# One encoder step on one core: row factors, the squares' output, the band norm's loads and block 2's operand splits are moved

## The chip, the cores and the metric

The kernel runs on one core of one Trainium2 chip. The time is device microseconds (us) of one execution of the whole program; beside it one execution was taken with the hardware profiler. TensorE (PE in the profile) does the matrix products, ScalarE (ACT), VectorE (DVE) and GpSimd (POOL) do elementwise work, and SyncE (SP) issues the DMA transfers. Each engine executes its own instructions in a fixed order and waits on semaphores for the others.

## The reference

A one-layer encoder step over 2048 prompt rows and 32 sample rows of width 1024:

```python
a = rmsnorm(x, g_attn)
qa, ka, va, qb, kb, vb = split(a @ w_in)           # two groups of heads, 512 columns each
oa = diff_attention(qa, ka, va)                    # group A: 4 heads, two maps each, chunk-causal
ob = band_attention(qb, kb, vb)                    # group B: 8 heads, band of 9 chunks of 64 rows
h = x + concat(rmsnorm(oa, subln_g) * 0.2, rmsnorm(ob, out_norm_b)) @ w_out
h = h + square(relu(rmsnorm(h, g_mlp) @ w_up)) @ w_down
h = h + sigmoid(h @ w_ple_gate) * (p @ w_ple_proj)
y = rmsnorm(h, g_final)
```

All values are float32; keys and values are outputs too.

## The kernel before

**Tiling.** The rows are cut into four blocks of 512 (block 3 has 544, the 32 sample rows being its tail). Activations lie transposed: 128 features on the partitions, rows along the free dimension. Every operand of a product is kept as two parts, a first part (rounded by ScalarE, `hi`) and a second part (the remainder, `lo`, by GpSimd or VectorE); `split` at line 178 makes the two, and `mm3` at line 210 does three matmuls per product (lines 216 to 218). In the profile a weight's first part is `wh` or `piece`, its second part `wl` or `piece`, and the raw weight from memory `wr`.

**Order.** The Python program traces instructions one after the other. A planner then fixes each engine's order: it runs a simulated clock and gives each engine the ready instruction that was traced earliest (a block under `high_priority` counts as traced earlier). So a matmul of a later stage fills a gap of an earlier one, and the attention of one block has the projection of another beside it. What the planner takes for ready is simulated; on the chip an engine that reaches an instruction too early waits there, with everything behind it. `tc.issue_after(ins)` puts the instructions that its block traces on the engine of `ins` behind `ins`. `weave` (line 100) and `weave2` (line 89) trace one generator and let another do a step after each of its steps. Tiles with one `tag` share a ring of `bufs` buffers.

**Preparation (`prep`, line 359).** For each tile of 128 rows (a "turn"): load `x`; square it with a sum over the row (line 371, which writes its unused squares into `xt`); transpose the eight 128x128 squares of `x` through PSUM tiles `xp` (line 378); write the two parts `aH` and `aL` (lines 383 and 384); copy the transposes to `xt` (line 387), which goes to memory as `xT`; from the row sums make the factor `rcol` (`rsqrt`, lines 223 to 231), transpose it by TensorE (line 392, `rp`) and copy it to `rbt` (line 393), by which queries and keys are scaled later. Blocks 0 and 1 are prepared at the start, beside group A's value tiles (`vtile`, `vps`); blocks 2 and 3 later, under raised priority, beside group B's projection and attention. There `x`, `xt` and `st` have one buffer each, and the PSUM tiles `xp`, `rp`, `vps` and `qps` share a ring of two banks.

**Band norm (`onorm`, line 927).** The factor of the norm of `ob`: load the four 128-row pieces `oraw` of the block from memory (`raw_o`, a ring of three buffers), square them on ScalarE (lines 934 and 936), add on GpSimd; split the sum (`sh`, `sl`), sum over partitions with TensorE (`css`, line 1100), take the inverse root, store it as `rB`. For blocks 0 and 1 it is woven into `proj_a` (37 steps, counted from 0) at the steps that `ONP` gives: block 0 at steps 28 and 34, block 1 at 29 and 35. The later use is in `oload` (line 940), which loads `rB` for the pieces 4 to 7 of the out-projection's operand `oact`. For blocks 2 and 3 `ONQ` gives the steps.

**Operands of block 2 (`cparts`, line 1008).** The MLP of blocks 2 and 3 uses seven combinations of the quarters of the normed activation (`b11`, `b21`, `b22`, `t1` to `t4`). For each of four `k`: two loads `tmp`, two scalings (line 1021), three splits, four additions on VectorE (lines 1033 to 1036), four splits of the sums; all of that in one step of the generator. Two steps are woven into `outproj(3)`, two into `gate(0)` (whose products are `gps` and `pps`), followed there by the first step of `mlp7(2)`, which makes its first weight combinations (`lead`). The same code for block 3, `cstage`, already does the last four splits of `k` after the loads of `k + 1`.

Of the kernel before, what the change touches and what calls it, by code (L numbers as in the profile page):

```python
# [20 lines left out]
P = 128  # L21
# [54 lines left out]
JA0 = [(0, 1), (2, 3)]  # L76
JA1 = [(4, 5), (6, 7, 8)]
JB = [(0, 1), (2, 3), (4, 5), (6, 7, 8)]
ONP = (28, 1, 6)
ONQ = (8, 1, 1)  # L80
PW = 272


# [5 lines left out]
def weave2(main, sides, at):  # L89
    n = 0  # L90
    for _ in main:
        for i, side in enumerate(sides):
            if n in (at[0] + i * at[1], at[0] + i * at[1] + at[2]):
                next(side, None)
        n += 1
    for side in sides:
        drain(side)


def weave(main, side, step, i=0, n=1):  # L100
# [43 lines left out]
class Kern:  # L144
# [33 lines left out]
    def split(self, hi, lo, raw, hi_eng="act", lo_eng="pool"):  # L178
        nc = self.nc
        if hi_eng == "act":  # L180
            nc.scalar.activation(hi, raw, AF.Copy)  # L181
        else:
            nc.vector.tensor_copy(hi, raw)
        if lo_eng == "pool":
            self.pool_tt(lo, raw, hi.bitcast(F32), ALU.subtract)
        else:
            nc.vector.tensor_tensor(lo, raw, hi.bitcast(F32), op=ALU.subtract)
# [171 lines left out]
    def prep(self, b, acts, pp, mm, tag, first=None):  # L359
        nc = self.nc  # L360
        aH, aL = acts[b]
        for i, (c0, n) in enumerate(toks(b)):
            t0 = 512 * b + c0
            x = pp.tile([P, D], F32, tag="x", name="x")
            self.dma(x[:n], self.xsrc(t0, n))
            if first is not None:
                first()
                first = None
            xt = pp.tile([P, 8, P], F32, tag="xt", name="xt")
            st = pp.tile([P, 1], F32, tag="st", name="st")  # L370
            nc.scalar.activation(
                xt[:n].rearrange("p a b -> p (a b)"), x[:n], AF.Square, accum_out=st[:n]
            )
            for h in range(2):
                xp = mm.tile([P, 4, P], F32, tag=tag, name="xp")
                for k in range(4):
                    kk = 4 * h + k
                    nc.tensor.transpose(xp[:, k, :n], x[:n, kk * P : kk * P + P], self.ident[:n, :n])
                for k in range(4):
                    kk = 4 * h + k  # L380
                    g = self.g_attn[:, kk : kk + 1]
                    hi, lo = aH[:, kk, c0 : c0 + n], aL[:, kk, c0 : c0 + n]
                    nc.scalar.activation(hi, xp[:, k, :n], AF.Copy, scale=g)
                    nc.vector.scalar_tensor_tensor(
                        lo, xp[:, k, :n], g, hi.bitcast(F32), op0=ALU.mult, op1=ALU.subtract
                    )
                nc.vector.tensor_copy(xt[:, 4 * h : 4 * h + 4, :n], xp[:, :, :n])
            self.dma(self.xT[:, :, t0 : t0 + n], xt[:, :, :n])
            r = self.rcol[:n, 4 * b + i : 4 * b + i + 1]
            self.rsqrt(pp, st[:n], 1, 1.0 / D, EPS, nc.vector, "r1", n, out=r)  # L390
            rp = mm.tile([P, 512], F32, tag=tag, name="rp")
            nc.tensor.transpose(rp[:, :n], r.broadcast_to([n, P]), self.ident[:n, :n])
            nc.scalar.activation(self.rb[b][:, c0 : c0 + n], rp[:, :n], AF.Copy)
            yield

    def ktok(self, b):
        if b < 3:
# [526 lines left out]
        self.dma(t, self.oT[:, k, t0 : t0 + n])  # L924
        return t

    def onorm(self, b, wk, ps, tag, dst):
        nc = self.nc
        n, t0 = BN[b], 512 * b
        sq = wk.tile([P, BLK], F32, tag="acc", bufs=2, name="sqacc")[:, :n]  # L930
        for k in range(4, 8):
            raw = self.raw_o(wk, k, t0, n)
            if k == 4:
                nc.scalar.activation(sq, raw, AF.Square)
            else:
                nc.scalar.activation(raw, raw, AF.Square)
                self.pool_tt(sq, sq, raw, ALU.add)
        yield from self.colnorm2(sq, b, 1.0 / 512, wk, ps, tag, dst, [])

    def oload(self, b, wk, up, out):  # L940
# [67 lines left out]
    def cparts(self, b, wk, cs, out, r):  # L1008
        nc = self.nc
        n, t0 = BN[b], 512 * b  # L1010
        m = n // 2
        names = ("b11", "b21", "t2", "t1", "t3", "b22", "t4")
        ops = {x: [cs.tile([P, 4, 272], F32R, tag="cs", name="cs")[:, :, :m] for _ in range(2)] for x in names}
        out[b] = ops
        for k in range(4):
            c = []
            for i in range(2):
                tmp = wk.tile([P, BLK], F32, tag="tmp", bufs=self.nt, name="tmp")[:, :n]
                kk = k + 4 * i
                self.dma(tmp, self.hS[:, kk, t0 : t0 + n])  # L1020
                nc.vector.scalar_tensor_tensor(
                    tmp, tmp, self.g_mlp[:, kk : kk + 1], r, op0=ALU.mult, op1=ALU.mult
                )
                c.append((tmp[:, :m], tmp[:, m:]))
            (b11, b12), (b21, b22) = c
            raw = {"b11": b11, "b21": b21, "b22": b22, "t3": b22, "t1": b12, "t2": b11, "t4": b21}

            def parts(*which):
                for x, e in which:
                    self.split(ops[x][0][:, k], ops[x][1][:, k], raw[x], "act", e)  # L1030

            parts(("b11", "pool"), ("b21", "dve"), ("b22", "dve"))
            nc.vector.tensor_tensor(b22, b22, b12, op=ALU.subtract)
            nc.vector.tensor_tensor(b12, b12, b11, op=ALU.subtract)
            nc.vector.tensor_tensor(b11, b22, b11, op=ALU.add)
            nc.vector.tensor_tensor(b21, b21, b11, op=ALU.subtract)
            parts(("t2", "dve"), ("t1", "dve"), ("t3", "dve"), ("t4", "pool"))
            yield

    def cstage(self, b, up, out, r):  # L1040
        nc = self.nc
# [414 lines left out]
    def run(self):  # L1456
        tc, nc, a = self.tc, self.nc, self.a
        with ExitStack() as top:
# [24 lines left out]
            with ExitStack() as x:  # L1483
                pp = opened(x, "pp0", 3, side="right")
                wv = opened(x, "wv0", 1, side="right")
                acts = {b: self.actpair() for b in HALVES[0]}
                for b in HALVES[0]:
                    self.rows(b, sg)
                units = []

                def first():
                    self.consts(cp)

                ring = Rings((ps_s, "s"), (ps_t, "tp"))
                todo = [(b, i) for b in HALVES[0] for i in range(4)]
                gen = (y for b in HALVES[0] for y in self.prep(b, acts, pp, ring, "s", first if b == 0 else None))
                next(gen)
                units.append(self.vunits(0, 0, pool=wv))
                next(gen)
                units.append(self.vunits(0, 1, pool=wv))  # L1500
                self.gains(cp)
                for b, i in todo:
                    for c in range(2):
                        self.vtile(b, i, 0, c, units[c], acts, sg, mm)
                    next(gen, None)
            ppx = ExitStack()
            pp = opened(ppx, "pp", 1)
            self.rawp = Rings((self.wp, "wr"), (opened(ppx, "wr3", 1), "wr"))
# [43 lines left out]
                for b in HALVES[1]:  # L1552
                    yield from self.proj((b,), 0, acts, sg, mm, tp, vs=(), gs=range(GS, 4))

            weave2(proj_a(), [self.onorm(b, wq, mm, "mm", self.rB) for b in HALVES[0]], ONP)
            s12.close()
            self.small = False
            sq_ = ExitStack()
# [65 lines left out]
            with ExitStack() as x:  # L1624
                act = Sized(opened(x, "acth", 2), BLK, True)
                weave(self.outproj(2, wk, oa[2], md, acc[2]), self.oload(3, wk, act, oa), 1, 0, 2)
                g = self.outproj(3, wk, oa[3], md, acc[3])
                made = []
                hp = self.hparts(0, wk, up, made)
                for _ in range(3):  # L1630
                    next(g)
                    next(hp, None)
                r2 = self.colnorm(acc[2][0], 2, 1.0 / D, wk, mm, "mm", None)
                c = self.cparts(2, wk, cs, ops, r2)
                weave(g, islice(c, 2), 1)
            hh = [opened(top, f"hh{i}", 1) for i in range(2)]
            h = hload(hh[0], BLK, 0)
            g = self.gate(0, h, up, None, md, wk, made[0])
            next(g)
            box = []  # L1640
            m = self.mlp7(2, hh[1], box, ops[2], wk, up, mm, md)
            weave(g, self.along(c, m), 1)
            f = self.final(0, h, up, fk, mm)
            for _ in range(2):
                next(m)
# [66 lines left out]
```

## Time and profile before

| | |
|---|---|
| median of 3 runs | 3151.15 us (3149.49 to 3156.91) |
| the profiled execution: its time, its span | 3146.42 us, 3144.6 us |
| mean granted TensorE clock | 0.985 |
| busy: VectorE, ScalarE, GpSimd | 1897.6, 1878.1, 1847.6 us (60%, 60%, 59%) |
| memory traffic | 539.27 MB, 172 GB/s over the span |

A row of the waits reads "engine, tile and line, what released it: total us, times, longest us". A row of the timeline reads "start, length, engine, line, operation, output and inputs, count, and in brackets the idle time before it with its releaser". A row of the windows gives, for a stretch, its length, then busy time and number of instructions of PE, PEld, DVE, ACT and POOL, the granted TensorE clock, the DMA share and GB/s. A row of a tile's or line's instructions gives the least, median and greatest length in ns.

### The profile page before, as it was taken

The page shows a single profiled execution, that of the slowest core. Times are in us where ns is not written, and L with a number is a line of the kernel's source. Part 1 is how long each engine was busy: PE and PEld are TensorE (multiplying, and loading weights), DVE is VectorE, ACT ScalarE, POOL GpSimd, SP SyncE. Part 2 cuts the span into 40 slices and gives each one's busy share as a digit, 9 for nine tenths or more (in the row PEclk, how much of TensorE's full clock was granted, in tenths as well). Part 3 has the DMA queues.
Part 4 walks back from the last instruction along what each step waited for, and adds up shares of the span by engine and source line. Part 5 has one row for each costly group of instructions (what it writes and reads, how often), then busy time and mean ns, then how long its engine had stood idle before and what let it go on. Part 6 is the DMA issues. An engine that isn't in the chain of part 4 may idle for free. (4 is left out here: it accounts for less than half of the span.)

```text
span 3144.6 us, 52811 instructions
## 1 busy us (share of the span) xinstructions
PE 3011.4 (96%) x17913; PEld 2649.6 (84%) x17913; DVE 1897.6 (60%) x4596; ACT 1878.1 (60%) x4166; POOL 1847.6 (59%) x2496
## 2 busy tenths in 40 slices
PE   8999898999999999999999999999899999999998
PEld 7787786899977887878788888878788887999998
DVE  5157774645465654666756556535667885576653
ACT  6257775766676764776666656554555455554545
POOL 2357455332345644665655545667877888667674
PEclk9999999999999999999999999999999999999999
DMA  8788757986788746555564543437533446333231
GB/s 281 244 244 244 204 185 229 263 232 201 205 250 230 218 130 153 152 154 153 157 184 130 144 123 103 145 116 241 179 128 115 144 152 229 123 107 107 88 116 56
DMA packets 523287, 539.27 MB, mean 171 GB/s; under 512 B 38749, under 2 KB 401569, under 8 KB 523017
## 3 DMA queue, kind: packets, MB, share of 16 engines
q1 hardware_dynamic: 523016, 535.89, 57.5%
q8 instruction: 142, 2.33, 0.3%
q14 instruction: 129, 1.05, 0.1%
HBM read 421.97 MB, written 117.75 MB: 172 GB/s over the span
## 5 line engine op out<-in xcount | busy, mean ns | idle before, releaser
L176 POOL TENSOR_TENSOR wl<-wr,wh 128x256 fp32r<-128x256 f32 x648 | 475.6, 766 | 354.8 <-ACT wh L181 315.7
L181 ACT ACTIVATE piece<-wr 128x512 fp32r<-128x512 f32 x406 | 246.1, 626 | 272.7 <-PE ups L217 113.1
L176 POOL TENSOR_TENSOR piece<-wr,piece 128x256 fp32r<-128x256 f32 x404 | 327.4, 837 | 99.7 <-ACT piece L181 86.4
L181 ACT ACTIVATE wh<-wr 128x1024 fp32r<-128x1024 f32 x228 | 241.2, 1058 | 171.7 <-PE qps L217 40.7
L166 POOL TENSOR_TENSOR wl<-wr,wh 128x256 fp32r<-128x256 f32 x264 | 199.4, 787 | 194.1 <-ACT wh L181 183.9
L216 PE MATMUL dps<-uh,piece 128*128 128x272 f32 (+1 forms) x768 | 247.0, 325 | 7.5 <-ACT piece L181 3.2
L166 POOL TENSOR_TENSOR piece<-wr,piece 128x256 fp32r<-128x256 f32 x280 | 237.0, 878 | 26.9 <-ACT piece L181 21.5
L218 PE MATMUL dps<-uh,piece 128*128 128x272 f32 (+1 forms) x768 | 247.8, 325 | 1.6 <-POOL piece L166 1.3
L217 PE MATMUL dps<-ul,piece 128*128 128x272 f32 (+1 forms) x768 | 247.8, 323 | 0.0
L216 PE MATMUL ups<-cs,piece 128*128 128x256 f32 (+1 forms) x864 | 246.0, 285 | 1.0 <-DVE r L1232 1.0
L217 PE MATMUL ups<-cs,piece 128*128 128x256 f32 (+1 forms) x864 | 245.3, 284 | 0.0
L218 PE MATMUL ups<-cs,piece 128*128 128x256 f32 (+1 forms) x864 | 245.2, 284 | 0.0
L216 PE MATMUL qps<-aH,wh 128*128 128x512 f32 (+1 forms) x640 | 231.2, 361 | 7.3 <-ACT kn L506 4.0
L218 PE MATMUL qps<-aH,wl 128*128 128x512 f32 (+1 forms) x640 | 229.5, 359 | 0.0
L217 PE MATMUL qps<-aL,wh 128*128 128x512 f32 (+1 forms) x640 | 228.5, 357 | 0.0
L1173 DVE TENSOR_TENSOR h<-h,dps 128x512 f32<-128x512 f32 x256 | 174.3, 683 | 80.9 <-PE dps L218 75.4
L1221 DVE TENSOR_TENSOR h<-h,dps 128x272 f32<-128x272 f32 (+1 forms) x384 | 189.3, 515 | 51.8 <-PE dps L218 50.8
L216 PE MATMUL dps<-uh,wh 128*128 128x512 f32 x512 | 207.8, 406 | 9.4 <-DVE h L1173 5.7
L216 PE MATMUL ups<-cH,wh 128*128 128x512 f32 x512 | 202.8, 396 | 2.1 <-ACT cH L181 1.1
L638 PE MATMUL s<-ka,q 128*128 128x512 f32 (+3 forms) x768 | 187.2, 345 | 15.9 <-ACT e L652 7.1
L218 PE MATMUL dps<-uh,wl 128*128 128x512 f32 x512 | 201.7, 394 | 0.5 <-POOL wl L166 0.4
L217 PE MATMUL ups<-cL,wh 128*128 128x512 f32 x512 | 201.2, 393 | 0.0
(317 smaller groups left out, 9634.2 us busy)
## 6 DMA issues: line engine op xcount, KB each, us to landing
wr<-w_up SPq DMA_DIRECT2D x128, 512.0 KB, 4.0
wr<-w_down SPq DMA_DIRECT2D x128, 512.0 KB, 3.8
wr<-w_in SPq DMA_DIRECT2D x74, 512.0 KB, 5.1
q<-qS SPq DMA_DIRECT2D x128, 256.0 KB, 5.4
v<-vSa SPq DMA_DIRECT2D x64, 512.0 KB, 3.9
ka<-kS SPq DMA_DIRECT2D x32, 512.0 KB, 8.9
wr<-w_out SPq DMA_DIRECT2D x32, 512.0 KB, 4.7
wr<-w_ple_gate SPq DMA_DIRECT2D x32, 512.0 KB, 4.3
```

What stands on the lines that cost most here:

```text
L166: nc.gpsimd.tensor_tensor(out[:, sl], a[:, sl], b[:, sl], op=op)
L176: nc.gpsimd.tensor_tensor(out[:, sl], a[:, sl], b[:, sl], op=op)
L181: nc.scalar.activation(hi, raw, AF.Copy)
L216: nc.tensor.matmul(ps, lh, rh, start=start and i == 0, stop=False)
L217: nc.tensor.matmul(ps, lh, rl, start=False, stop=False)
L218: nc.tensor.matmul(ps, ll, rh, start=False, stop=stop and i == n - 1)
L638: nc.tensor.matmul(s, q[:, m, hl, P * qi : P * qi + nr], kt[:, m, k0 - kb : k0 - kb + n], start=hl == 0, stop=hl == 1)
L1173: nc.vector.tensor_tensor(hv, hv, ps, op=ALU.add)
L1221: nc.vector.tensor_tensor(hv, hv, ps, op=ALU.add)
```

## The change

Four edits. (1) In `prep` the transposition of the row factor and its copy are traced a turn later, after the next turn's work, and the last one after the loop; the first stage drains its generator for it. (2) The squares of a full tile are written into the part of `aL` that the turn will fill afterwards, no longer into `xt`. (3) `onorm` for blocks 0 and 1 loads three pieces at one step, squares them at the next and loads the fourth there, squares that one at the third and goes on as before; each group of squares is put behind the ScalarE instruction of the last split traced. `ONP` becomes steps 27, 28, 29 and 35 for block 0 and 29, 30, 31 and after the end for block 1; `ONQ` in its new form names the same steps as before. (4) `cparts` gives back after the loads and scalings of each `k` and traces the last four splits of `k` after those of `k + 1`; its eight steps are woven as four into `outproj(3)`, two into `gate(0)`, then a step of `mlp7`, then the rest. Nothing is computed more or less often.

```diff
-ONP = (28, 1, 6)
-ONQ = (8, 1, 1)
+ONP = (27, 2, (0, 1, 2, 8))
+ONQ = (8, 1, (0, 1))
@@ weave2
-            if n in (at[0] + i * at[1], at[0] + i * at[1] + at[2]):
+            if n - at[0] - i * at[1] in at[2]:
@@ split
-            nc.scalar.activation(hi, raw, AF.Copy)
+            self.last = nc.scalar.activation(hi, raw, AF.Copy)
@@ prep
+        late = []
+
+        def row(r, c0, n):
+            rp = mm.tile([P, 512], F32, tag=tag, name="rp")
+            nc.tensor.transpose(rp[:, :n], r.broadcast_to([n, P]), self.ident[:n, :n])
+            nc.scalar.activation(self.rb[b][:, c0 : c0 + n], rp[:, :n], AF.Copy)
...
+            junk = aL[:, :, c0 : c0 + P] if n == P else xt
             nc.scalar.activation(
-                xt[:n].rearrange("p a b -> p (a b)"), x[:n], AF.Square, accum_out=st[:n]
+                junk[:n], x[:n].rearrange("p (a b) -> p a b", b=P), AF.Square, accum_out=st[:n]
             )
...
-            rp = mm.tile([P, 512], F32, tag=tag, name="rp")
-            nc.tensor.transpose(rp[:, :n], r.broadcast_to([n, P]), self.ident[:n, :n])
-            nc.scalar.activation(self.rb[b][:, c0 : c0 + n], rp[:, :n], AF.Copy)
+            while late:
+                row(*late.pop())
+            late.append((r, c0, n))
             yield
+        row(*late.pop())
@@ onorm
+        raws = [(k, self.raw_o(wk, k, t0, n)) for k in range(4, 4 + ahead)]
+        if ahead:
+            yield
+            with self.tc.issue_after(self.last.ins):
+                for k, raw in raws:
+                    add(k, raw)
+            raws = [(k, self.raw_o(wk, k, t0, n)) for k in range(4 + ahead, 8)]
+            yield
+            with self.tc.issue_after(self.last.ins):
+                for k, raw in raws:
+                    add(k, raw)
+        else:
+            for k in range(4, 8):
+                add(k, self.raw_o(wk, k, t0, n))
@@ cparts
+        late = ()
         for k in range(4):
...
-            parts(("b11", "pool"), ("b21", "dve"), ("b22", "dve"))
+            parts(k - 1, *late)
+            yield
+            parts(k, ("b11", b11, "pool"), ("b21", b21, "dve"), ("b22", b22, "dve"))
...
-            parts(("t2", "dve"), ("t1", "dve"), ("t3", "dve"), ("t4", "pool"))
+            late = (("t2", b11, "dve"), ("t1", b12, "dve"), ("t3", b22, "dve"), ("t4", b21, "pool"))
             yield
+        parts(3, *late)
@@ run
+                drain(gen)
...
-            weave2(proj_a(), [self.onorm(b, wq, mm, "mm", self.rB) for b in HALVES[0]], ONP)
+            weave2(proj_a(), [self.onorm(b, wq, mm, "mm", self.rB, 3) for b in HALVES[0]], ONP)
...
-                weave(g, islice(c, 2), 1)
+                weave(g, islice(c, 4), 1)
...
-            weave(g, self.along(c, m), 1)
+            weave(g, chain(islice(c, 2), islice(m, 1), c), 1)
```

More of the change, by code (lines that the diff above doesn't have):

```diff
@@ L925, in raw_o, with onorm @@
         return t
-    def onorm(self, b, wk, ps, tag, dst):
+    def onorm(self, b, wk, ps, tag, dst, ahead=0):
         nc = self.nc
@@ L930, in onorm, with add @@
         sq = wk.tile([P, BLK], F32, tag="acc", bufs=2, name="sqacc")[:, :n]
-        for k in range(4, 8):
-            raw = self.raw_o(wk, k, t0, n)
+        def add(k, raw):
             if k == 4:
-                nc.scalar.activation(sq, raw, AF.Square)
+                ins = nc.scalar.activation(sq, raw, AF.Square)
             else:
-                nc.scalar.activation(raw, raw, AF.Square)
+                ins = nc.scalar.activation(raw, raw, AF.Square)
                 self.pool_tt(sq, sq, raw, ALU.add)
+            return ins
+        raws = [(k, self.raw_o(wk, k, t0, n)) for k in range(4, 4 + ahead)]
[12 more added lines that the diff above has]
+                add(k, self.raw_o(wk, k, t0, n))
         yield from self.colnorm2(sq, b, 1.0 / 512, wk, ps, tag, dst, [])
@@ L1014, in cparts, with parts @@
         out[b] = ops
+        def parts(k, *which):
+            for x, raw, e in which:
+                self.split(ops[x][0][:, k], ops[x][1][:, k], raw, "act", e)
+        late = ()
         for k in range(4):
@@ L1025, in cparts @@
             (b11, b12), (b21, b22) = c
[L1026 to L1030, printed above, removed]
-            parts(("b11", "pool"), ("b21", "dve"), ("b22", "dve"))
+            parts(k - 1, *late)
+            yield
+            parts(k, ("b11", b11, "pool"), ("b21", b21, "dve"), ("b22", b22, "dve"))
             nc.vector.tensor_tensor(b22, b22, b12, op=ALU.subtract)
```

## The prediction

> **What bounds the kernel now.** I read the page first, then TensorE's list of waits over the whole run, then the timeline and windows around each wait that one of the four edits touches.
>
> ```profile
> span 3144.6 us, 52811 instructions
> ...
> PE 3011.4 (96%) x17913; PEld 2649.6 (84%) x17913; DVE 1897.6 (60%) x4596; ACT 1878.1 (60%) x4166; POOL 1847.6 (59%) x2496
> ```
>
> TensorE is busy for 96% of the span and no other engine passes 60%. The change takes no matmul away, so all that can be won lies in the 3144.6 - 3011.4 = 133.2 us in which TensorE stands idle, and in matmuls that run slowly after such a stop. TensorE's waits over the run, the rows that the edits touch:
>
> ```profile
> PE gps L216 <- ACT piece L181: 6.5, 1, 6.5
> ...
> PE rp L392 <- DVE xt L387: 4.6, 3, 2.8
> ...
> PE qps L216 <- ACT kn L506: 4.0, 1, 4.0
> ...
> PE rp L392 <- DVE rcol L231: 2.8, 4, 1.4
> ...
> PE gps L218 <- POOL piece L176: 1.6, 1, 1.6
> ```
>
> Together 19.5 us, 0.6% of the run. The reader is to see that each is a place of its own: the two `rp` rows are preparation, `qps` after `kn` is the band norm, the `gps` rows are the gate of block 0. The times below are summed against the profiled execution (3146.42 us, its span and 1.8 us around it); it lies 4.7 us under the median 3151.15, and I carry the difference over to the median.
>
> **The row factor a turn later, first stage.** No instruction is added or taken: 17 transposes and 17 copies move. The wait for `rcol` (2.8 us, four times; the list of the first 77 us alone has the same row) goes, because a turn later the factor has long been made. The PSUM tile that the transpose takes is the same in number and comes at the same place of the turn, so no more than that goes. I take -2.5 us; bounds -2.8 and 0.
>
> **The squares, both stages.** The line of the squares over the run, ScalarE's waits from 300 to 530 us, and TensorE's in the same stretch:
>
> ```profile
> L371 ACT ACTIVATE xt<-x x17: 1043/1061/1134, 4.4 to 502.2; 128x1024 f32<-128x1024 f32 x16, 32x1024 f32<-32x1024 f32 x1
> ...
>   DMA xT<-xt: 15.0, 9
> ```
>
> ```profile
> ACT xt L371 <- DMA xT<-xt: 12.7, 6, 4.5
> ```
>
> ```profile
> PE s L638 <- ACT e L652: 6.9, 8, 2.9
> ```
>
> ScalarE stands 15.0 us, nine times, in front of the squares until the copy `xt` of an earlier turn has left for memory. With the squares in `aL` that wait moves to VectorE's copy at line 387, which in a turn comes after the transposes and parts, by when the transfer should be over. What is late next is whatever ScalarE holds up for TensorE. In the first stage that is 15.0 - 12.7 = 2.3 us of ScalarE, of which I count 0.5 us for TensorE. Later it is 12.7 us, and what TensorE waits for exponentials in that stretch is 6.9 us at most, caused in part by VectorE. I take -1.5 us there; bounds -6.9 and 0. The squares' new window has gaps between its runs of 128. ScalarE writes such a window at line 865 and one without gaps at line 506:
>
> ```profile
> 866.00 0.60 ACT L865 ACTIVATE pb<-tpb 128x512 fp32r<-128x512 f32 x1 [0.31 <-PE tpb L857]
> ...
> 867.21 0.59 ACT L506 ACTIVATE kn<-ktp 128x512 f32<-128x512 f32 x1
> ```
>
> 0.60 against 0.59 us: a square stays at 1061 ns. What it costs that the squares now write `aL` is the last rival below.
>
> **The row factor in blocks 2 and 3.** The timeline around the longest `rp` wait:
>
> ```profile
> 486.84 0.47 DVE L231 TENSOR_TENSOR rcol<-rsy,rsv 128x1 f32<-128x1 f32 x1
> ...
> 496.90 0.48 PE L392 MATMUL rp<-ident,rcol 128*128 128x128 f32 x1 [2.82 <-DVE xt L387]
> ...
> 497.75 0.79 PE L216 MATMUL qps<-aH,wh 128*128 128x512 f32 x1 [0.37 <-ACT rbt L393]
> ```
>
> `rcol` was ready at 487.3, 9.6 us before the transpose. What it waits for is its PSUM bank: `xt` at line 387 is the last reader of the `xp` tile that held it. A later transpose leaves that bank to the next tile in the ring, here `qps`, which must wait for the same copy. So of these 4.6 us I count nothing as won; bounds -4.6 and 0. This is where I expect the change to do less than its wording suggests.
>
> **The band norm.** The timeline of SyncE, ScalarE and TensorE, and the windows behind it:
>
> ```profile
> 627.63 0.32 SPq L157 DMA_DIRECT2D oraw<-oT x1
> ...
> 630.49 0.63 ACT L936 ACTIVATE oraw<-oraw 128x512 f32<-128x512 f32 x1 [3.48 <-DMA oraw<-oT]
> ...
> 631.79 0.60 PE L216 MATMUL qps<-aH,wh 128*128 128x272 f32 x1 [3.99 <-ACT kn L506]
> ```
>
> ```profile
> 631.80:634.70 2.90, 2.90 (x13) 2.90 (x14) 1.20 (x5) 2.90 (x8) 0.81 (x2) 0.50 1.08 295
> 634.70:637.90 3.20, 3.20 (x26) 3.20 (x26) 1.21 (x3) 1.72 (x4) 0.00 (x0) 1.00 1.02 263
> ```
>
> ScalarE came to the square of the fourth piece at 627.0, before its load was issued, and stood 3.48 us; `kn`, queued behind it, held a PSUM bank, and TensorE stood 3.99 us. After that stop the granted clock was 0.50 for 2.9 us: 13 matmuls where the next 3.2 us held 26, so about 2.9 - 13 x 3.2/26 = 1.3 us more. The place costs 5.3 us. With loads a step ahead of the squares it goes.
>
> Against it stands what becomes late. SyncE and TensorE at the end of the projection:
>
> ```profile
> 892.28 0.40 PE L1100 MATMUL css<-sh,ones_r 128*128 128x512 f32 x1
> ```
>
> ```profile
> 895.02 0.87 SPq L157 DMA_DIRECT2D qS<-qh  x2
> ...
> 901.34 0.33 SPq L157 DMA_DIRECT2D rB<-r  x1
> ...
> 905.88 0.87 SPq L157 DMA_DIRECT2D kS<-qh  x2
> ...
> 913.01 0.32 SPq L157 DMA_DIRECT2D rb<-rB  x1
> ```
>
> Block 0's sum over partitions moves from step 34 to step 35. The steps' stores (`qS` at 895.02, `kS` at 905.88) stand 10.9 us apart, so `css` comes near 903 and `rB`, 9.1 us behind it, near 912, about when its load (913.01) is issued now. That load then waits for the store to land, and the load, the out-projection's operands 4 to 7 and the transfers queued behind it on SyncE come some 2 us late (bounds 0 and 10.9), while the attention of group B alone does not fill TensorE. Eight squares join ScalarE's queue behind the projection's splits; the adds and the split of the sum wait for them, and nothing that TensorE needs before step 35. Sum -5.3 + 2.3 = -3 us; bounds -5.3 and +5.6.
>
> **Block 2's operands.** The tile `tmp` from 2195 to 2290 (who waited for it; its splits), the timeline, and two sets of windows:
>
> ```profile
> L187 DVE TENSOR_TENSOR cs<-tmp,cs x20: 409/942/962, 2212.1 to 2267.6; 128x256 fp32r<-128x256 f32 x20
> ...
>   ACT cs L181: 20.1, 14
> ```
>
> ```profile
> 2258.63 0.62 ACT L181 ACTIVATE piece<-wr 128x512 fp32r<-128x512 f32 x1
> ...
> 2259.30 0.80 PE L216 MATMUL gps<-hu,piece 128*128 128x512 f32 x1 [6.46 <-ACT piece L181]
> ```
>
> ```profile
> 2259.30:2262.00 2.70, 2.70 (x6) 2.05 (x7) 2.70 (x7) 1.99 (x5) 1.86 (x3) 0.50 0.00 0
> 2262.00:2265.00 3.00, 3.00 (x13) 2.40 (x12) 2.97 (x5) 1.94 (x6) 3.00 (x4) 0.86 0.60 180
> ...
> 2268.00:2272.00 4.00, 4.00 (x19) 3.28 (x18) 2.08 (x4) 3.60 (x7) 4.00 (x6) 1.00 0.09 16
> ```
>
> ```profile
> sum 66.80, PE 58.17 PEld 46.04 DVE 44.95 ACT 39.91 POOL 58.24; mean PE 11.63 PEld 9.21 DVE 8.99 ACT 7.98 POOL 11.65
> ```
>
> ScalarE waits 20.1 us, 14 times, for VectorE's sums before it can split them, and the gate's weight split (2258.63) stands in that queue; TensorE waits 6.46 us for it and 1.6 us for GpSimd's part of another. Then 19 matmuls take 5.7 us where 19 at full clock take 4.0: 1.7 us more. The place costs 6.5 + 1.6 + 1.7 = 9.8 us. With the splits a step behind, the sums are done when ScalarE comes to them. What is late next is GpSimd: the last row, the sum of five windows from 2219.2 to 2286 (the gate of block 0), has it busy for 58.24 us, as long as TensorE (58.17). Were all 9.8 us to go, GpSimd would have 58.24 us of work in about 57. Part may run on into the MLP. I take half, -5 us; bounds -9.8 and 0.
>
> The Trainium skill ("SBUF — State Buffer", on the shared port pair) says that a VectorE instruction with two SBUF inputs and a GpSimd instruction that reads SBUF lock each other out for a whole instruction. The trace agrees in kind: the same second-part subtraction takes 409 ns at the least and 942 in the median. By that rule the change moves none of this load out of the stage, and the term would be nearer 0 than -9.8.
>
> **Sum.** -2.5 - 0.5 - 1.5 + 0 - 3 - 5 = -12.5 us: 3146.42 - 12.5 = 3133.9 for a profiled execution, 3151.15 - 12.5 = 3138.65, so 3139 us as a median (0.4% faster).
>
> **Rivals.** (a) *GpSimd and the PSUM ring keep what the edits free.* The gate's wait turns from ScalarE to GpSimd and gives 1 us, the squares give nothing, the band norm keeps its 3, the first stage 2: -6, 3145 us. For it: 58.24 against 58.17, and the bank wait at 496.90. Against it: GpSimd itself stands idle 8.6 of those 66.8 us. (b) *Everything goes through*: -2.8 - 2.3 - 6.9 - 5.3 - 9.8 = -27.1, 3124 us; the case begins halfway, at about 3131. Against it: several waits have a second one close behind. (c) *The planner lays new waits where old ones went*, since it re-orders every engine around four places by its own simulated times: about 0, 3151 us. For it: the present stops are themselves of that kind, such as a square that ScalarE reaches before its load is issued. (d) *Slower: the squares join the path.* They become writers of `aL`, so the second parts wait for them, and if the planner's bookkeeping can't tell their window with gaps from the neighbouring turns' columns, the value tiles wait too, and each square for earlier value tiles. Price: 17 x 1.06 = 18.0 us if all stand on TensorE's path, with the waits at `xT` unmended and the band norm and gate giving their 8: +10, 3161 us. It makes the change a loss of 0.3% from 17 squares on and eats the 8 us from 8 on. Against it: `pb` is written through windows with gaps too, and TensorE's waits that the edits touch don't name it.
>
> **How the numbers follow.** 0.3% is 9.45 us, about what a measurement of this kernel can tell from no change: faster is below 3141.7, slower above 3160.6. Forecast 0.55 (0.45 of it below 3141.7), (a) 0.20, (b) 0.08, (c) 0.09, (d) 0.08. Faster 0.45 + 0.08 = 0.53; same 0.10 + 0.20 + 0.09 = 0.39; slower 0.08. For 8 in 10 the range reaches from 3128, within (b), to 3153, past (c) but not to (d).
>
> **What would show it.** In the profile after: no wait of `rp` for `rcol`; no idle time of ScalarE at line 371 for `xT`, little at line 387; a wait for `xt` at line 387 still there, under `rp`, `qps` or `vps`; no wait of line 936 for `oraw` that TensorE feels, and `css` of block 0 near 903 with `ops` waiting a little longer near 917; the 6.5 us in front of `gps` down to 3 or less, with POOL as releaser. The prediction is wrong if TensorE's idle time of 133.2 us does not fall by 8 to 18 us, or falls at other places than these.

## The result, and the profile after

| | before | after |
|---|---|---|
| median | 3151.15 us (3148.14 to 3156.91) | 3201.37 us (3199.18 to 3205.73) |
| ratio of the times, 95% interval | | 1.0158 (1.0147 to 1.0169) |
| span of the profiled execution | 3144.6 us | 3199.6 us |
| mean granted TensorE clock | 0.985 | 0.974 |

The change makes the kernel 50 us slower. The first rows of the page after, to be held against the two that open the prediction:

```profile
span 3199.6 us, 52843 instructions
...
PE 3033.9 (95%) x17913; PEld 2666.2 (83%) x17913; DVE 1896.0 (59%) x4596; ACT 1879.2 (59%) x4166; POOL 1837.1 (57%) x2496
```

The same 17913 matmuls take 3033.9 - 3011.4 = 22.5 us longer, and TensorE's idle time grows from 133.2 to 3199.6 - 3033.9 = 165.7 us, by 32.5. So of 55 us between the two spans, three fifths are new stops and two fifths matmuls that run longer, in line with the granted clock, which fell from 0.985 to 0.974. TensorE's waits over the whole run of the kernel after (what released it: total us, times, longest us):

```profile
PE dps L216 <- DVE h L1201: 12.3, 13, 2.3
PE s L647 <- ACT e L661: 11.6, 10, 7.1
PE sb L844 <- DVE stb L847: 11.5, 10, 3.3
...
PE gps L216 <- ACT piece L181: 5.0, 1, 5.0
...
PE rp L366 <- DVE xt L395: 4.2, 3, 2.8
PE gps L216 <- DVE sig L1398: 3.6, 1, 3.6
```

The reader is to see two things. Of the rows that the prediction quoted, `rp` after `rcol` and `qps` after `kn` are gone, `gps` after `piece` has shrunk from 6.5 to 5.0, and `rp` after `xt` is still there (4.2 against 4.6). The gate gains nothing, though, since a wait of 3.6 for `sig` now stands beside the 5.0. And the largest rows are now ones that no edit names: `s` and `sb` in attention, `dps` in the MLP.

**Where the time goes.** Every run has the same matmuls, in partly another order. Counting each at the usual duration of its form gives a common scale of work done, and the times at equal work can be compared (to about 2 us where the order differs). Against a control (the kernel before, run again, below) the kernel after is behind by

| matmul work done (time in the control) | us behind |
|---|---|
| end of the value and key projection (677 us) | 10.3 |
| just before the sums of the band norm (883 us) | 11.1 |
| out-projection and attention of group B under way (1107 us) | 32.2 |
| attention of group A beside the MLP (1360 us) | 48.7 |
| the same (1493 us) | 38.8 |
| before block 2's operands (2207 us) | 41.7 |
| behind the gate of block 0 (2387 us) | 45.5 |
| end | 43.5 |

Some 4 of the 10 us that come back between 1360 and 1493 us are a stop that the control also has, only later. The main loss begins where the band norm's sum stands. SyncE and TensorE of the kernel after at that place (start, length, engine, line, operation, tiles, idle time before it):

```profile
917.01 0.39 PE L1128 MATMUL css<-sh,ones_r 128*128 128x512 f32 x1
...
923.02 0.79 PE L1128 MATMUL css<-sh,ones_r 128*128 128x512 f32 x1 [1.97 <-ACT kn L515]
```

```profile
933.89 0.54 SPq L157 DMA_DIRECT2D rB<-r  x1
...
938.66 0.32 SPq L157 DMA_DIRECT2D rb<-rB  x1
...
945.50 0.33 SPq L157 DMA_DIRECT2D oraw<-oT  x1
```

Before, `css` of block 0 stood at 892.28, `rB` at 901.34 and `rb` at 913.01: the sum is 25 us later, the store 33, the load 26, of which 11 are the lag that was there already. Later stops follow. The longest of the run, on SyncE, ScalarE and TensorE:

```profile
1245.93 3.16 SPq L157 DMA_DIRECT2D wr<-w_up  x2
```

```profile
1257.83 1.06 ACT L181 ACTIVATE wh<-wr 128x1024 fp32r<-128x1024 f32 x1 [8.83 <-DMA wr<-w_up]
1258.79 0.67 ACT L661 ACTIVATE e<-s,nm 128x512 f32<-128x512 f32 x1
```

```profile
1259.60 1.22 PE L647 MATMUL s<-ka,q 128*128 128x512 f32 x2 [7.08 <-ACT e L661]
```

TensorE's row names an exponential. But `e` had only stood in the queue behind the split of a weight whose load was issued 3 us before ScalarE came to it. TensorE's stop is the wait for a load, and no edit touches that load.

### The profile page after: what moved, and what is told of

The parts are those of the page before. It is cut to its first block, busy times and chain, and to the rows that moved or that the text cites. A ratio compares the mean times of both kernels' runs of the same rounds, so it can differ in the third digit from the quotient of the medians.

```text
span 3199.6 us, 52843 instructions
## 1 busy us (share of the span) xinstructions
PE 3033.9 (95%) x17913; PEld 2666.2 (83%) x17913; DVE 1896.0 (59%) x4596; ACT 1879.2 (59%) x4166; POOL 1837.1 (57%) x2496
## 5 line engine op out<-in xcount | busy, mean ns | idle before, releaser
L653 DVE TENSOR_REDUCE nm<-s 128x1 f32<-128x512 f32 (+3 forms) x256 | 147.4, 587 | 95.6 <-PE s L647 94.3
```

What stands on the lines that cost most here:

```text
L653: nc.vector.tensor_reduce(nmx, s, axis=AX.X, op=ALU.max, negate=True)
```

## The experiments

The first theory from this comparison (N in the expectations) is that the band norm's edit alone opens the main loss. Its rival P is that the loss belongs to no edit in particular: the planner re-orders whatever is changed and lays new stops. All ratios are against the kernel before, run between them on the same chip; its median lay at 3156 to 3160 us there, so us are worked out as (ratio - 1) x 3157. Of the edits' diffs only the choice of parts is shown; the parts themselves are in the change.

**Each edit alone.** The four parts of the diff, one at a time.

```diff
e1_norm    only ONP, ONQ, weave2, self.last and onorm
e2_row     only row(), late and drain(gen)
e3_junk    only junk = aL[:, :, c0 : c0 + P] if n == P else xt
e4_cparts  only cparts and the two weaves around it
```

> Only the band norm's edit (loads a step ahead, steps 27/28/29/35 and 29/30/31/end). Theory N: this edit alone opens the gap between 880 and 1450 us of the changed kernel, about +35 us, so 3180 to 3192 us (+30 to +40), with the next sum over partitions after the band norm's (the out-projection's) some 20 us later than its 990.7 us before, and no gap before 880 us or after 2000 us. Rival P (the planner re-orders whatever is changed, and the gap belongs to the sum of the edits): within 10 us of before, 3141 to 3161 us. Rival C (the prediction's price was right and something else opens the gap): -3 us, 3145 to 3151 us.

> Only the row factor a turn later. By the prediction's term -2.5 us (3148 to 3151). By theory N nothing that can be measured (-3 to +4 us; the changed kernel was 4 us late by its first 45 us of matmul work, which may be this edit or the squares'). By rival P a gap of 10 us or more somewhere after 500 us, 3160 us or more.

> Only the squares' unused output into the second parts. By the prediction's terms -2 us (3149); if the first 4 us that the changed kernel loses are this edit's, the gap is there in the first 60 us and the sum is 0 to +8 us (3151 to 3159); if the rival of the prediction holds in which the squares become writers of the second parts and stand on the path, +8 us or more (3159 to 3169). By rival P +10 us or more at other places than preparation.

> Only the splits of block 2's operands a step behind. By the prediction's term -5 us (3141 to 3151). If the changed kernel's gap of 11 us between 2034 and 2420 us is this edit's: +8 to +14 us (3159 to 3165), in the out-projection of block 3 and the gate of block 0. If that gap is carried over from the band norm through the planner's order: 0 to -5 us.

| kernel | median us | ratio, 95% interval | us against before |
|---|---|---|---|
| e1_norm | 3168.47 | 1.0035 (1.0022 to 1.0048) | +11 |
| e2_row | 3160.85 | 1.0019 (1.0002 to 1.0035) | +6 |
| e3_junk | 3170.89 | 1.0050 (1.0032 to 1.0069) | +16 |
| e4_cparts | 3163.93 | 1.0025 (1.0013 to 1.0038) | +8 |

No edit gives a gain, and my theory N missed: the band norm alone costs a third of what it was to cost, a little more than the 10 us of P. The squares' +16 is what P, or rival (d), was to show, the operand splits' +8 what was expected of a gap of their own, and the row factor's +6 lies between N and P. The four sum to +41 of the +50. What each does is in its own trace.

*Row factor.* TensorE's waits for `rp` in the first 100 us, of the control and then of the edit alone:

```profile
PE rp L392 <- DVE rcol L231: 2.5, 3, 1.8
```

```profile
PE rp L366 <- DVE xt L394: 5.0, 2, 2.9
```

The wait for the factor goes, and the wait for the bank that `xt` still reads takes its place, twice as long. That is what the prediction saw for blocks 2 and 3 and did not see for the first stage. The kernel's lag there is within the scatter of the control's kind (below), so the size stays open between 0.6 and 11 us. In the whole change this bank wait is absent from the first 100 us; in its place a value tile waits 4.9 us for ScalarE's split of a weight (`vps` after `wh`).

*Squares.* With the squares in `aL`, ScalarE's 13.0 us of waits for `xT` (control) are down to 4.8, one wait. A lag of 11 us opens at 322 us; half of it comes back by 390 us, and with other small stops of the stage it is 13 us at the end of the projection. SyncE, GpSimd, ScalarE and TensorE of that kernel:

```profile
318.20 0.53 SPq L157 DMA_DIRECT2D ba<-dba  x1
```

```profile
326.99 0.14 POOL L330 MEMSET ba<- 64x64 f32 x1 [5.68 <-DMA ba<-dba]
327.10 0.72 POOL L231 TENSOR_TENSOR rsy<-rsy,rsv 128x256 f32<-128x256 f32 x1
```

```profile
327.85 0.38 ACT L223 ACTIVATE rsv<-ss 128x256 f32<-128x256 f32 x1 [6.50 <-POOL rsy L231]
328.13 0.27 ACT L394 ACTIVATE rbt<-rp 128x128 f32<-128x128 f32 x1
```

```profile
328.45 0.58 PE L216 MATMUL vps<-wh,aH 128*128 128x256 f32 x1 [5.92 <-ACT rbt L394]
```

Read from the bottom: a value tile waits for a bank, the bank for ScalarE's copy of a row factor, that copy for an inverse root ahead of it in ScalarE's queue, the root for GpSimd, and GpSimd for a mask of attention whose load was issued 8.8 us before. Nothing in this chain is a square, and the squares' own line has no engine waiting for it in the whole run. In the control the mask is loaded at 311.60 and filled at 315.78, and there is no such chain. Nor does it come with the squares in every order: in the whole change GpSimd stands even longer for this mask (9.8 us), and TensorE has no such stop there.

*Operand splits.* This kernel has every matmul at its old place; on the other engines the order is the old one up to some 2200 us. TensorE's waits from 2230 to 2335 us, of the control and of the edit alone:

```profile
PE gps L216 <- ACT piece L181: 7.9, 2, 7.6
```

```profile
PE gps L216 <- ACT piece L181: 5.1, 1, 5.1
PE gps L216 <- DVE sig L1373: 3.5, 1, 3.5
PE ups L216 <- DVE r L1235: 2.0, 1, 2.0
PE css L1103 <- DVE u L1235: 2.0, 1, 2.0
```

The stop at the gate is split in two (5.1 and 3.5 for 7.9), and two new ones of 2.0 us stand in the MLP. VectorE's row ahead of them:

```profile
2313.89 0.69 DVE L1262 TENSOR_TENSOR wr<-wr 128x512 f32<-128x512 f32 x1 [3.28 <-DMA wr<-w_up]
```

Again an engine came to a load too early; `u` and `r`, which the MLP waits for, stand behind it in VectorE's queue. In the profile this kernel loses 3 us on the control from 2190 to 2420 us; the rest of its +8 shows at no place, since its order ahead of that is the control's.

So N fell as far as it goes alone, and P is borne out in part. What N left open is why the whole change loses so much more at the band norm's place. Theory L: the price is the lateness of the sums, and through it of `rB` and the out-projection's operands. Its rival, Q: the price is the loads and squares held behind the splits.

**Lateness, and the control.**

```diff
c0_before      the kernel before, unchanged
n1_css_later   e1_norm, but
-            with self.tc.issue_after(self.last.ins):
n2_css_kept    e1_norm, but
-ONP = (27, 2, (0, 1, 2, 8))
+ONP = ((26, 27, 28, 34), (28, 29, 30, 35))
a1_no_norm     after, with onorm, ONP and ONQ as before
```

> The kernel before itself, once more, as a control: a ratio whose interval holds 1 (0.997 to 1.003), and a profile that says how far one profiled execution lies from another of the same program. The kernel with the operand splits alone executes the same order as before on every engine until about 2190 us, and its profile was 10 us behind that of before by 1450 us; if that is scatter of executions, this profile ends anywhere from 3145 to 3165 us. If it is a real cost of that edit, this profile keeps within 3 us of before's and ends near 3145.

> The band norm's edit with the same steps but without putting the squares behind the splits: every engine has the order of before until the first block's sum over partitions, which comes a step later as in the full edit. Theory L (the edit's cost is the late sum: its factor is stored some 14 to 20 us later, and the out-projection's operands 4 to 7 with it): no gain at 632 us, a loss of 10 to 14 us between 880 and 960 us, 3159 to 3170 us (+8 to +14). By the prediction's term for it, +2 us. Rival Q (the cost comes from the loads and squares held behind the splits, with the load buffers taken for longer): 0 to +3 us.

> The band norm's edit with all its steps one earlier for block 0 (26, 27, 28 and 34) and block 1 at 28, 29, 30 and 35, so that both sums over partitions keep the steps of before, with the squares still behind the splits. Theory L: the gain at 632 us stays (about -5) and the loss after 880 us goes: -6 to 0 us against before. Rival Q: the loss stays, +6 to +14 us.

> The changed kernel without the band norm's edit. If costs simply add (row, squares and operand splits alone were +6, +16 and +8 us): +30, about 3185 us. If the squares' +16 is a stop that only their planner order makes, and the row edit moves it: +12 to +18 us, 3168 to 3174, with the loss in front of 520 us and at the gate, and none of the three stops of 5 to 7 us that the changed kernel has between 1250 and 1404 us. If those stops are there too, they belong to the other edits.

| kernel | median us | ratio, 95% interval | us against before |
|---|---|---|---|
| c0_before | 3157.90 | 1.0001 (0.9991 to 1.0012) | 0 |
| n1_css_later | 3166.80 | 1.0021 (1.0008 to 1.0034) | +7 |
| n2_css_kept | 3150.01 | 0.9977 (0.9968 to 0.9987) | -7 |
| a1_no_norm | 3175.50 | 1.0057 (1.0042 to 1.0072) | +18 |

The control's span is 3156.1 us, 11.5 over that of the profile on which the prediction rests. Two profiles of the same order differ by some 5 us in the first 300 us alone, so lags under that say nothing.

In n1 and n2 theory L is borne out against Q: up to the first sum, n1's order is that of before on every engine, so its 7 us (3 to 11, a little under the 8 to 14 that I expected) are the price of a sum one step later, with no square held behind a split. With the sums at their old steps the same loads and squares, a step earlier, make the kernel 7 us faster than before. The gain has its place: TensorE's wait from 600 to 660 us in the control, and nothing of the kind in n2 (its `css` stands at 893.28, in the control at 893.20):

```profile
PE qps L216 <- ACT kn L506: 4.6, 1, 4.6
```

The way that L names, through `rB`, is only a part of the price. In n1 VectorE stands 1.9 us for `rb`, and TensorE 2.7 us for the operand behind it; but the control has a stop of 2.2 us for an operand too, whose own load is late. What n1 has besides is a stop at the sum itself: block 1's sum now comes after the end of the projection, and waits for ScalarE.

```profile
913.60 0.50 PE L1114 MATMUL css<-sh,ones_r 128*128 128x512 f32 x1 [1.98 <-ACT kn L506]
```

n2 gets 6.7 us back on the control between 584 and 677 us; the prediction had 5.3.

**The whole change with its sums kept, and variants.**

```diff
a2_css_kept     after, with ONP as in n2_css_kept
n3_css_sooner   n2_css_kept, ONP = ((26, 27, 28, 31), (28, 29, 30, 33))
j1_own_tile     before, and in prep
+            junk = pp.tile([P, 8, P], mybir.dt.bfloat16, tag="jk", bufs=1, name="jk")
-                xt[:n].rearrange("p a b -> p (a b)"), x[:n], AF.Square, accum_out=st[:n]
+                junk[:n], x[:n].rearrange("p (a b) -> p a b", b=P), AF.Square, accum_out=st[:n]
k1_halves       n2_css_kept, cparts as after, and
-                weave(g, islice(c, 2), 1)
+                weave(g, islice(c, 4), 1)
-            weave(g, self.along(c, m), 1)
+            weave(g, self.along((next(c, None) for _ in c), m), 1)
```

> The changed kernel, all four edits, with the band norm's steps at 26, 27, 28, 34 and 28, 29, 30, 35, so that the sums over partitions keep their old steps. Theory L (the late sums cost the changed kernel its loss from 890 us on, the stops in the attention of block 2 included, since those appear only with them): below the changed kernel without the band norm's edit (3175.5) by the 7 us that the edit gives when its sums are kept, 3165 to 3172 us. Rival: the squares held behind the splits and the other edits' new order disturb each other wherever the sums stand: 3185 to 3201 us.

> The band norm's edit alone with loads and squares at 26, 27, 28 and 28, 29, 30 and the sums over partitions three and two steps before their old places (31 and 33). One step later cost 7 to 14 us. Theory L with the sums still on the path of the out-projection: a further gain, 3140 to 3147 us, with less lost between 880 and 960 us than in the kernel that keeps the sums (3150.0). If the out-projection's start is bound by something else once the sums are in place: 3147 to 3153 us.

> The kernel before with the squares' unused output in a tile of its own (bfloat16, one buffer), neither in the transposes' tile nor in the second parts. If the squares cost 16 us because they became writers of the second parts: -3 to +2 us against before. If the cost was the stop behind the mask (GpSimd standing 5.7 us in front of its fill of the loaded mask, with the inverse root behind it), it follows the planner's order: gone where that fill stands behind its load by more than 8 us, there where it doesn't, with the wait of the squares for the transfer of the transposes (15 us of ScalarE) gone either way.

> The band norm's edit with its sums kept, and of the operand splits' edit only the part in the out-projection of block 3 (half steps there; in the gate whole steps, and the MLP's first step where it was). If what costs in the operand splits' edit is the part in the gate (the MLP's first weights and the last k changing places): within 3 us of the kernel without it, 3147 to 3153. If the half steps cost: 3153 to 3158.

| kernel | median us | ratio, 95% interval | us against before |
|---|---|---|---|
| a2_css_kept | 3174.19 | 1.0048 (1.0030 to 1.0066) | +15 |
| n3_css_sooner | 3154.33 | 0.9991 (0.9979 to 1.0002) | -3 |
| j1_own_tile | 3157.00 | 0.9995 (0.9986 to 1.0004) | -2 |
| k1_halves | 3152.31 | 0.9986 (0.9976 to 0.9996) | -4 |

One line of step numbers takes the whole change from +50 to +15 us (3174.19 is a little over the 3165 to 3172 that I expected). The expectations speak of three stops of 5 to 7 us between 1250 and 1404 us; in TensorE's rows they are one of 7.1, a pair of 2.1 and 1.8 at 1318 us and one of 5.0. The first two are gone with the sums kept, and the last is 3.6 us, where the control has 3.3. Sums still earlier give nothing more: once in place they don't bind. In a tile of their own the squares cost nothing and gain nothing that can be measured, though ScalarE's wait for `xT` is gone; its waits at that line are 15.6 us for `x` instead. So it is the second parts as target that cost, and as no engine waits for the squares there, by the order they lead to; that last step is read from the trace, and no run tests it. And the half steps in the out-projection cost at most a few us (-4 against -7 without them, the intervals overlapping); by elimination, what costs in the operand splits is the part in the gate, where the MLP's first weights change places.

**Lateness or held squares.** The sums cost 7 us alone and far more in the whole change.

```diff
s1_free_squares  after, but
-            with self.tc.issue_after(self.last.ins):
s2_ahead_both    n2_css_kept, and
-ONQ = ((8, 9), (9, 10))
+ONQ = ((5, 6, 7, 8), (7, 8, 9, 10))
-                weave2(m, [self.onorm(i, wk, mm, "mm", self.rB) for i in HALVES[1]] if b == 0 else [], ONQ)
+                weave2(m, [self.onorm(i, wk, mm, "mm", self.rB, 1) for i in HALVES[1]] if b == 0 else [], ONQ)
```

> The changed kernel with its late sums, but the squares not put behind the splits (they go early, as before). Theory L in its plain form (lateness alone): 3190 to 3201 us, with stops of 5 to 7 us again between 1250 and 1404 us. If the late sums cost their 7 us and the rest comes from the squares and load buffers held at 866 us: 3178 to 3186 us (the changed kernel without the band norm's edit, 3175.5, and some 7 us), and those stops are gone.

> The band norm's edit with its sums kept (3150.0), and for blocks 2 and 3 also loads a step ahead of the squares, one piece at steps 5 and 7, three more at 6 and 8, the sums at 8 and 10. In the control ScalarE stands 4.12 us for the second piece of block 3 and TensorE 3.3 us for the exponentials' split queued behind it, 6.4 us with the slow clock. If that goes and nothing else moves: 3142 to 3147 us. If the planner's new order lays a stop elsewhere in the attention of blocks 2 and 3: 3150 us or more.

| kernel | median us | ratio, 95% interval | us against before |
|---|---|---|---|
| s1_free_squares | 3181.88 | 1.0074 (1.0058 to 1.0091) | +23 |
| s2_ahead_both | 3152.12 | 0.9979 (0.9968 to 0.9989) | -7 |

Without the band norm's edit the other three cost +18. The late sums with free squares make that +23 (s1), held squares with all steps one earlier +15 (a2): both lie within the noise of +18. Late sums and held squares together make it +50 (after). Neither alone does it. With both, the squares stand at 866 to 892 us, right in front of the sum that needs them, and `css` comes 23 us behind the point that the control passes at 883 us; with the squares free it is 20 there, with the sums kept 10. Between 883 and 1107 us of the control that costs the kernel after some 21 us, s1 7 and a2 none.

Where the 21 us go can be read off. The first 4 are the held squares' own. ScalarE stands at a square of block 1 whose load is late; exponentials (`eb`) stand behind it, and TensorE's scores `sb` wait for VectorE behind those. The band norm's edit alone has the same stop (3.0 and 3.2 us) and loses 5 us there, which is about what it costs over n1; n1, s1, n2 and a2 have none there. So Q has its share too.

```profile
890.13 0.63 ACT L945 ACTIVATE oraw<-oraw 128x512 f32<-128x512 f32 x1 [3.02 <-DMA oraw<-oT]
```

```profile
895.94 1.43 PE L844 MATMUL sb<-kbt,q 128*128 128x320 f32 x4 [2.60 <-DVE stb L847]
```

About 7 follow around the second `css` and the first operands, as in n1 and s1. The largest piece, 8 us, is again a load that an engine reached too early: VectorE stands for `tmp`, from which an operand of the MLP is made.

```profile
1092.29 0.75 DVE L1027 SCALAR_TENSOR_TENSOR tmp<-tmp,g_mlp_s,rl 128x512 f32<-128x512 f32 x1 [4.59 <-DMA tmp<-hS]
```

```profile
1093.70 2.29 PE L896 MATMUL ob<-pb,vbt 128*128 128x512 f32 x5 [5.68 <-DVE stb L851]
```

The stop of 7.1 us is absent in s1; one of 4.8 us remains. Why the later order puts the load of `w_up` 3 us before its split, or that of `tmp` so late, was not followed further. The planner decides it, and neither stop is there in s1 or a2.

s2 takes the stop of the same form in block 3 away (the control has 3.3 us of it) and is 11 us ahead of the control near 1406 us, then gives 6 back at 1465 us, where TensorE stands 2.74 us for `relu`. So it ends where n2 does. n2 and s2 beat both kernels; n2 does it with less.

## Why the prediction was wrong

**The bound** was read rightly: what can be won lies in TensorE's idle time and the slow matmuls behind it. That same reading says that a stop can be added as well as taken away, at 4 to 9 us each with its clock, against terms of 0.5 to 5 us.

**Row factor, first stage** (-2.5, lower bound -2.8, upper bound 0). The row of 2.8 us is gone. Alone, the edit put a bank wait of 5.0 in its place and gave +6 us (0.6 to 11); in the whole change a wait of 4.9 for a weight's split stands there. The step "comes at the same place of the turn, so no more than that goes" failed: in the edit alone the tile is taken while `xt` is still reading the bank that it needs.

**Row factor, blocks 2 and 3** (0, the bank wait stays). Right: 4.2 us after, 4.6 before.

**Squares** (-0.5 and -1.5). The wait for `xT` went as predicted, but what came next was not TensorE: j1, which has the edit without the second parts, gives -2 us (-4 to +1). In the kernel after, the waits of ScalarE at the squares' line:

```profile
  DMA x<-x_prompt: 10.9, 7
  DMA xT<-xt: 4.9, 1
```

15.0 us in nine waits for `xT` have become 4.9 in one, that of the 32 sample rows, whose square still writes `xt`. But before, ScalarE stood 2.6 us for `x` at this line, and now 10.9. The step "what is late next is whatever ScalarE holds up for TensorE" left out the load of `x`: ScalarE's idle time in front of the squares fell only from 17.6 to 16.1 us. What cost 16 us alone is the order that the new target brings, not the 18 us of squares on TensorE's path of rival (d): the chain at 322 us has no square in it.

**Band norm** (-5.3 + 2.3). The first number held: 6.7 us came back (n2). The second is the step that failed most. I priced the sum's step as 10.9 us of lateness that the attention would nearly hide, at some 2 us. Measured, the sum a step later costs 7 us with the squares free (n1), within the bounds of 0 and 10.9 but three times the value I took. With the squares held, all steps of the edit one later cost 18 (e1 against n2), over the bound, and in the whole change 35 (after against a2); there the loads and squares move with the sums, so that this is not the price of the sums alone. The prediction even had the squares' place ("nothing that TensorE needs before step 35"); it did not ask what else stands behind them in ScalarE's queue when a load is late (890.13 us), nor what they hold up at step 35 itself.

**Block 2's operands** (-5). Who waited for the tile `tmp` in the kernel after, from 2220 to 2340 us:

```profile
  ACT cs L181: 20.6, 16
```

It was 20.1 us in 14 waits. The prediction read all of them as waits for VectorE's sums. By line (1021 before, 1052 after) a good part are waits for the scalings, which the edit doesn't take away. ScalarE's row for them before, from 2195 to 2290 us, and after, from 2220 to 2340:

```profile
ACT cs L181 <- DVE tmp L1021: 8.0, 5, 4.7
```

```profile
ACT cs L181 <- DVE tmp L1052: 10.7, 5, 4.7
```

That leaves 12.1 us for the sums before and 10.0 after. "The sums are done when ScalarE comes to them" failed: the splits moved, but half of ScalarE's waiting is still for sums, and what the sums lost the scalings gained. By the rule of the Trainium skill ("SBUF — State Buffer", on the shared port pair) that the prediction set beside this term, none of the load was to leave the stage. ScalarE's waits agree with that; VectorE's second-part subtraction doesn't, as its median fell from 942 to 614 ns and ScalarE waited as long as before. The term came out at +8 us (4 to 12), past its upper bound of 0; its profile alone shows 3 of them, between the gate and two stops further on in the MLP.

**The rivals.** The one that came true is (c): the planner lays new waits elsewhere. It had 0.09 and a price of about 0, as if new waits could at most make up for the old ones. That was the error in size: three of the four edits re-order every engine, for hundreds of us each, and the fourth every engine but TensorE. Stops that can be read off as loads that an engine reached too early are, in the kernel after, the square at 890, `tmp` at 1092 and `w_up` at 1258, and in the squares' edit alone the mask at 322. The kernel before had some of the kind as well. One is in block 3's band norm, which the change leaves as it was; it is the stop at 632 over again, and grew from 3.3 us (control) to 5.0 (ScalarE, then TensorE, of the kernel after):

```profile
1402.60 0.63 ACT L945 ACTIVATE oraw<-oraw 128x512 f32<-128x512 f32 x1 [6.67 <-DMA oraw<-oT]
```

```profile
1403.77 0.58 PE L736 MATMUL o<-pH,v 128*128 128x256 f32 x1 [4.98 <-ACT pH L729]
```

## What to carry to other kernels

A step moved later is priced by what its consumers wait for, not by the gap that it opens in a queue: here one line of step numbers is worth 35 us in the whole change, and the wait that the edit removes 7. Where a planner orders every engine from a traced order, an edit's size is not the size of its waits: try the parts singly, keep the one whose trace shows the gain at its place, and look in the others for the load that an engine now reaches too early. And when TensorE's row of waits names an engine, follow that engine's queue back to the first instruction that waited: in most of the long stops followed here it was a load that had nothing to do with the tile named.

## What the runs showed of the hardware

The granted clock fell after a stop of 1.97 us. Windows of the kernel after, around the second `css` (length, then busy time and count of PE, PEld, DVE, ACT and POOL, granted clock, DMA share, GB/s):

```profile
917.00:921.00 4.00, 3.43 (x22) 2.52 (x20) 4.00 (x13) 3.92 (x8) 2.78 (x4) 1.00 0.77 223
921.00:923.10 2.10, 0.13 (x2) 0.09 (x1) 2.10 (x3) 2.10 (x7) 2.08 (x2) 0.97 0.99 219
923.00:926.00 3.00, 2.98 (x6) 1.88 (x7) 1.80 (x7) 2.89 (x7) 0.08 (x1) 0.50 1.03 301
```

Three microseconds at 0.50 follow, and `css` takes 0.79 us where the one before took 0.39. So a stop of 2 us can cost three quarters as much again (3 us at half clock lose 1.5). Over the run, TensorE's idle time shows some three fifths of what the change cost (32.5 of 55 us).

The same load landed at different times: the mask's, of 128x256, 8.7 us after its issue at 318.20 in the squares' edit alone, 4.1 us after its issue at 311.60 in the control. The DMA share was about 1 in both stretches (1.08 from 318 to 327 us, 1.01 from 310 to 316), so that share doesn't tell which load will be late.
